# Eighteen weight splits of the Hyena stage move from GpSimd to VectorE

## The chip, the cores and the metric

The kernel runs on one core of a Trainium2 chip. The metric is the time of one execution on the device in microseconds (us). The kernel before takes 3416.87 us, the median of three runs that lie between 3413.32 and 3423.29 us. One execution was taken with the hardware profiler; it took 3412.15 us itself, and its span, from the first to the last recorded instruction, is 3410.4 us.

## The reference

The kernel computes two layers of a diffusion backbone over 1024 latent tokens and 256 context tokens, each of 1024 channels. The first layer runs a bidirectional mLSTM (4 heads) beside a Hyena group of 512 channels; the second is a 2-D neighbourhood attention with 16 heads. Each layer ends in an MLP. What the change touches is the projection `h @ w_in` of the first layer, cut to this:

```python
def project(h, rope):
    q, k, v, o, g, hy = jnp.split(h @ w_in, cuts, axis=-1)
    ...
def combine(hm, o, hy, dtype):
    u, x1, x2 = jnp.split(short_conv(hy, conv_w, conv_b), 3, axis=-1)
    filt = hyena_filters(l_, f_w1, f_b1, f_w2, f_b2, f_w3, f_freq)
    b_out = hyena(u, x1, x2, filt, hy_d)
def hyena(u, x1, x2, filt, dskip):
    z = u
    for o, gate in enumerate((x1, x2)):
        z = gate * (bidir_long_conv(z, filt[:, o, 0], filt[:, o, 1]) + dskip[o] * z)
    return z
```

The long convolution goes through a Fourier transform along the tokens: multiply by the filter's spectrum, transform back, multiply by the gate.

## The kernel before

**Precision by splitting.** A float32 weight tile of 128 x 1024 numbers is written as a sum of a high part `wh`, which is the tile rounded to the TensorE format fp32r, and a low part `wl`, the remainder. Activations are split in the same way. `gemm` (L170) forms each product of three matmuls: L177 and L178 read `wh`, L179 reads `wl`.

**A weight tile's way.** `wload` (L150) asks SyncE's queue (SP) to load 512 KB into `wr` (L155), of which there is one buffer. `split` (L110) then has ScalarE (ACT) cast `wr` into `wh` (L112), and an engine given as `e` subtract `wh` from `wr` into `wl` (L113); with no engine given that is VectorE (DVE). `wh` and `wl` have two buffers each, so a cast waits until TensorE (PE) is done with the tile before last. The next load into `wr` waits until the subtraction has read it. SP's queue is worked in order: what stands behind that load, such as the loads of filter spectra into `Gt` (L618, two buffers) and the stores of staged results (L1050), waits with it.

**The Hyena stage.** It lies between about 205 and 605 us of the span. For each of four groups of 128 channels, three calls of `hy_block` (L578) project u, x1 and x2 with one weight tile each and apply the short convolution: ACT evicts the product (L590, L591), DVE adds the two outer taps (L108). `decimate` (L597) transposes on PE (L605). `hyena_fft` (L609) transforms with small matmuls (L613), and DVE does the butterflies, the multiplication by the spectrum in `Gt` and the butterflies back (L96, L108, tiles `q`, `b`, `s`, `n`). `hyena_gate` (L627) transforms back on PE (L640), and DVE multiplies by the gate out of PSUM (`big<-psf,big`). `gates` (L654) computes the mLSTM gates once, with a weight tile of its own. To give PE more to do, `filler` (L1041) projects some of the mLSTM's q, k, v, o ahead of time: five of its sixteen tiles in this stage, eleven in the mLSTM stage behind it.

**Order.** All instructions are unrolled. A planner sets the order on every engine when the kernel is built, from estimated durations, dependences, buffers and priorities; each engine then runs its own list strictly in that order. The weight loads of `hy_block` have priority "hy" (1000), those of `gates` 60 and those of `filler` 150.

**Who makes `wl` before.** `W_E` (L69) is GpSimd (POOL). It is given to the loads of `hy_block`, `gates`, `filler` and the output projection (L1129, L1161): 12 + 1 + 16 + 8 + 2 = 39 tiles. All other weight tiles, 105 of the same group, are split on DVE. In the Hyena stage POOL has little else to do; the filters that are computed ahead of it also use POOL for some butterflies.

Of the kernel before, what the change touches and what calls it, by code (L numbers as in the profile page):

```python
# [27 lines left out]
def kernel(ctx: ExitStack, tc: tile.TileContext, A, out):  # L28
    nc = tc.nc
    V, S, T, G = nc.vector, nc.scalar, nc.tensor, nc.gpsimd  # L30
# [8 lines left out]
    def mk(pool, shape, tag, bufs, dt=F32):  # L39
        cnt[0] += 1  # L40
        return pool.tile(shape, dt, tag=tag, bufs=bufs, name=f"{tag}_{cnt[0]}")
# [18 lines left out]
    def pr(k):  # L60
        k = HP.get(k, k)
        return ExitStack() if k is None else tc.high_priority(k)
# [3 lines left out]
    PS0, PS1 = dict(g=2, f=2, m=1, t=2, q=1), dict(g=4, f=3, m=1)  # L66
    PS2 = dict(g=3, f=3, m=1, q=1)
    FS, FH, FM = (0, 0, 0), (0, 1, 0, 1, 0, 1, 0, 2), (3, 4, 4)
    W_E = G  # L69

    def psum(**split):

# [16 lines left out]
    def n2(shape=None):  # L89
        return mk(base, shape or [P, 512], "n2", 4)  # L90
# [16 lines left out]
    def stt(o, a, s, b, op0, op1):  # L107
        return V.scalar_tensor_tensor(out=o, in0=a, scalar=s, in1=b, op0=op0, op1=op1)  # L108

    def split(hi, lo, x, e=None):  # L110

        S.copy(hi, x)  # L112
        (e or V).tensor_tensor(out=lo, in0=x, in1=hi.bitcast(F32), op=ALU.subtract)  # L113
# [36 lines left out]
    def wload(at, src, e=None, ks=(0, 8), into=None):  # L150
        with pr(at):
            wp_ = wpool[0]
            raw = mk(wp_, [P, 8, P], "wr", 1)
            r = slice(*ks)
            nc.sync.dma_start(raw[:, r], src)  # L155
            if into is None:
                hi = mk(wp_, [P, 8, P], "wh", 2, F32R)
                lo = mk(wp_, [P, 8, P], "wl", 2, F32R)
            else:
                hi, lo = [mk(into[0], [P, 8 * P], t, into[2], F32R).rearrange("p (k c) -> p k c", c=P) for t in into[1]]  # L160
            split(hi[:, r], lo[:, r], raw[:, r], e)
        for f in msteps[:MS]:
            f()
        del msteps[:MS]
        return hi, lo
# [4 lines left out]
    def gemm(w, h, g, n, M=P, ks=range(8), tag="g"):  # L170

        hi, lo = w
        hh, hl = h
        ps = pt([P, 512], tag)
        ks = list(ks)
        for i, k in enumerate(ks):
            T.matmul(ps[:M, :n], hi[:, k, :M], hh[g][:, k, :n], start=(i == 0), stop=False)  # L177
            T.matmul(ps[:M, :n], hi[:, k, :M], hl[g][:, k, :n], start=False, stop=False)  # L178
            T.matmul(ps[:M, :n], lo[:, k, :M], hh[g][:, k, :n], start=False, stop=(i == len(ks) - 1))  # L179
        return ps  # L180
# [27 lines left out]
    def mod_steps(l, g, pool, bufs, tag):  # L208

        ps = [None]  # L210
        for i in range(16):
            def step(k=i % 8, c0=i // 8 * 256):
                if k == 0 and c0 == 0:
                    ps[0] = pt([P, 512], tag)
                w = mk(pool, [P, 8, P], bufs[0], bufs[1]).rearrange("p (j a) b -> p j (a b)", j=4)
                nc.sync.dma_start(w, A["w_mod"][l, k * P:(k + 1) * P, g * 2048:(g + 1) * 2048].rearrange("p (j c) -> p j c", j=4)[:, :, c0:c0 + 256])
                for j in range(4):
                    T.matmul(ps[0][32 * j:32 * j + 32, c0:c0 + 256], sil[:, k, :], w[:, j], start=(k == 0), stop=(k == 7))
                if k == 7 and c0:
                    mod_end(l, g, ps[0], tag)  # L220
            yield step
# [356 lines left out]
    def hy_block(eb, h, hc, wp):  # L578

        with pr("hb"):  # L580
            w = wload("hy", A["w_in"][eb], W_E)
            hy = mk(wp, [P, BIGN], "big", 5)
            V.memset(hy[:, 0:1], 0.0)
            V.memset(hy[:, 1025:1027], 0.0)
            V.memset(hy[:, 1283:1284], 0.0)
            s = mk(wp, [P, BIGN], "big", 5)
            for g, (t0, n) in enumerate(GR):
                ps = gemm(w, h, g, n)
                o = 1 + t0 if t0 < LAT else 3 + t0
                S.copy(hy[:, o:o + n], ps[:, :n])  # L590
                S.activation(s[:, t0:t0 + n], ps[:, :n], AF.Identity, scale=hc["cw"][:, eb, 1:2], bias=hc["cb"][:, eb:eb + 1])  # L591
            for t0, n, o in ((0, LAT, 0), (LAT, CTX, 1026)):
                for tap in (0, 2):
                    stt(s[:, t0:t0 + n], hy[:, o + tap:o + tap + n], hc["cw"][:, eb, tap:tap + 1], s[:, t0:t0 + n], ALU.mult, ALU.add)
            return s
# [58 lines left out]
    def gates(h, mp, keep):  # L654

        with pr("gt"):
            R = 104

            hi, lo = wload("ga", A["w_in"][12], W_E)
            S.copy(hi[:, :, 32:64], lo[:, :, 0:32].bitcast(F32))  # L660
            sel = mk(mp, [P, 8, P], "q4", 3)[:64, 0, :100]
            nc.scalar.dma_start(sel, A["gsel"])
# [18 lines left out]
            I, F, e, u1, ln, b, ml = [sm[:R, i] for i in range(7)]  # L681
# [30 lines left out]
            eb, emx, me, mp_ = [rows[:, i] for i in range(4)]  # L712
# [34 lines left out]
    def mlstm_consts(pool):  # L747
        rope = mk(pool, [P, 2, LAT], "rope", 1)
        nc.scalar.dma_start(rope, A["rope"])
        mask = mk(pool, [P, 2, P], "mmask", 1)  # L750
        nc.scalar.dma_start(mask, A["mmask"])
        hn = mk(pool, [P, 4], "hn", 1)
        nc.scalar.dma_start(hn, A["hnorm"])
        return rope, mask, hn
# [274 lines left out]
    def split_groups(h, k, src, gr):  # L1029
        for g, (t0, n) in enumerate(gr):  # L1030
            split(h[0][g][:, k], h[1][g][:, k], src[:, t0:t0 + n])
# [6 lines left out]
    h = new_h()  # L1038
    fill = [(hd, j) for hd in range(4) for j in range(4)]

    def filler(n, stage):  # L1041

        with pr("fb"):
            for hd, j in fill[:n]:
                w = wload("fl", A["w_in"][13 + 4 * hd + j], W_E)
                for g, (t0, n_) in enumerate(GR):
                    ps = gemm(w, h, g, n_)
                    st = stage()
                    S.activation(st[:, :n_], ps[:, :n_], AF.Copy, scale=128 ** -0.5 if j == 1 else 1.0)
                    nc.sync.dma_start(early[hd, j, :, t0:t0 + n_], st[:, :n_])  # L1050
            del fill[:n]
# [3 lines left out]
    with tc.tile_pool(name="hp", bufs=1, side="right") as hp:  # L1055
        hc = {}
        stage = lambda: mk(hp, [P, 512], "st", 1)
# [55 lines left out]
    with tc.tile_pool(name="gp", bufs=1, reuse_waits="tile", side="right") as gp:  # L1113
        cst = mlstm_consts(gp)
        with tc.tile_pool(name="ml", bufs=1, reuse_waits="tile") as ml:
            h2 = []
            for g in (1, 2):
                msteps.extend(mod_steps(0, g, ml, ("wm", 2), "n"))

            def load_mixed(k):  # L1120
                with pr("lm"):
                    m_ = mk(ml, [P, BIGN], "big", 13)
                    nc.sync.dma_start(m_[:, :NT], mixd[k])
                    split_groups(h2, k, m_, GR)

            def out1(d):

                with pr("o1"):
                    w = wload("wo1", A["w_out"][d][:, 0:6], W_E, (0, 6))  # L1129
                    for g, (t0, n) in enumerate(GR):  # L1130
                        xp = n2()
                        nc.sync.dma_start(xp[:, :n], A["xT"][:, d, t0:t0 + n])
                        ps = gemm(w, h2, g, n, ks=range(6))
                        stt(xp[:, :n], ps[:, :n], modT[0][:, 16 + d, int(g == 2):int(g == 2) + 1], xp[:, :n], ALU.mult, ALU.add)
                        nc.sync.dma_start(xs[:, d, t0:t0 + n], xp[:, :n])

            mlstm_head(0, gs, ml, cst, lambda k, t: nc.sync.dma_start(mixd[4 + k], t))
            filler(FM[0], n2)
            mlstm_head(1, gs, ml, cst, lambda k, t: nc.sync.dma_start(mixd[4 + k], t))
            filler(FM[1], n2)  # L1140
            last = []
            mlstm_head(2, gs, ml, cst, lambda k, t: nc.sync.dma_start(mixd[4 + k], t))
            filler(99, n2)
            h2.extend(new_h())
            for k in range(6):
                load_mixed(k)
            for d in range(FM[2]):
                out1(d)
            mlstm_head(3, gs, ml, cst, lambda k, t: split_groups(h2, 4 + k, t, GR))
            load_mixed(6)  # L1150
            for d in range(FM[2], 8):
                out1(d)
    gkc.close()
    cst = natten_consts(ctx.enter_context(tc.tile_pool(name="cn", bufs=1, side="right")))
    with tc.tile_pool(name="xg", bufs=1, reuse_waits="tile", side="right") as xp:
# [4 lines left out]
        h = new_h()  # L1160
        w2 = [wload("wo2", A["w_out"][d0:d0 + 4, :, 6:8].rearrange("d p k c -> p d k c"), W_E) for d0 in (0, 4)]  # L1161
        for g, (t0, n) in enumerate(GR):
            for d in range(8):
                hi, lo = [x[:, 2 * (d % 4):2 * (d % 4) + 2] for x in w2[d // 4]]
# [20 lines left out]
    with tc.tile_pool(name="nl", bufs=1, reuse_waits="tile") as nl, \  # L1185
# [29 lines left out]
        for d in range(8):  # L1215
            w = wload("ow1", A["w_o"][d][:, 0:7], E5, (0, 7))
            residual(xg, 1, 0, d, 0, gemm(w, h2, 0, 512, ks=range(7)), 512)
    with tc.tile_pool(name="xg1", bufs=1, reuse_waits="tile", side="right") as xp:
# [3 lines left out]
        hi, lo = wload("ow2", A["w_o"][:, :, 7].rearrange("d p c -> p d c"), E1)  # L1222
# [7 lines left out]
        for d in range(8):  # L1230
            w = wload("ow3", A["w_o"][d], E1)
# [136 lines left out]
```

## Time and profile before

| | before |
|---|---|
| median of three runs | 3416.87 us |
| profiled execution | 3412.15 us |
| its span | 3410.4 us |
| PE busy over the span | 3256.5 us |
| DVE busy over the span | 2056.0 us |
| POOL busy over the span | 355.8 us |
| `wl` made on POOL | 39 instructions, 134.0 us |
| `wl` made on DVE | 105 instructions, 127.5 us |

A row of a group of instructions gives line, engine, operation, output and inputs, shape, count, then busy time, the mean duration of one in ns, and the idle time of the engine just before them with what ended it. A row of the view in order of time gives the start and the duration in us, and in square brackets the idle time of the engine before it with what ended that. "psf", "psg" and "psm" are PSUM tiles. A row of the table of stretches gives, for each engine, busy time and count, then the granted TensorE clock, the share of the DMA engines and GB/s.

### The profile page before, as it was taken

Reading aid. Unit: us, or ns where it says so; the run is one execution under the profiler, and the core shown is the slowest. Engines: PE = TensorE matmul, PEld = TensorE weight load, DVE = VectorE, ACT = ScalarE, POOL = GpSimd, SP = SyncE. Lnnn points to the kernel's source line nnn. Section 1 sums busy time; section 2 is a strip of 40 time slices with the busy share of each in tenths; the row PEclk is TensorE's granted clock in tenths of the full one; section 3 lists DMA queues with packets and bytes.
Section 4 is the critical chain, followed back from the end, with each engine's and each line's share of the span. In section 5 each row is a group of like instructions: output and inputs, shape, how many; then the busy total and the mean of one; then the engine's idle time right before and its main releaser. Section 6 shows DMA issues by size and latency. Waiting matters only on the chain.

```text
span 3410.4 us, 45323 instructions
## 1 busy us (share of the span) xinstructions
PE 3256.5 (95%) x18044; PEld 2652.5 (78%) x18044; DVE 2056.0 (60%) x3655; ACT 1211.5 (36%) x2555; POOL 355.8 (10%) x295
## 2 busy tenths in 40 slices
PE   6889989999989999999999999999999899999999
PEld 4777878777877888788888777777777688888887
DVE  4858979366576445444454776666666755545444
ACT  5742222244343121211111476666665421111111
POOL 0341232101120000000000211111110200000000
PEclk8999999999999999999999999999999999999999
DMA  6432211775632121212111212221224211111111
GB/s 210 151 110 66 72 64 64 256 233 198 204 126 87 61 82 56 93 56 87 56 37 38 78 47 72 69 67 62 70 78 161 68 56 47 47 50 47 47 50 68
DMA packets 140878, 306.12 MB, mean 90 GB/s; under 512 B 12497, under 2 KB 74057, under 8 KB 139258
## 3 DMA queue, kind: packets, MB, share of 16 engines
q1 hardware_dynamic: 131018, 266.60, 23.8%
q0 software_dynamic: 6464, 28.84, 2.8%
q10 hardware_dynamic: 3184, 7.78, 0.7%
q8 instruction: 142, 2.33, 0.3%
q14 instruction: 70, 0.57, 0.1%
HBM read 255.93 MB, written 43.05 MB: 88 GB/s over the span
## 4 chain that ended last, share of the span: by engine, by line
PE 64%; DVE 5%; DMA 4%; ACT 3%; issue 1%; POOL 0%; ACTq 0%; SPq 0%; DVEq 0%; POOLq 0%
PE psg L177 10%; PE psg L178 10%; PE psg L179 10%; PE psf L312 8%; PE psf L313 8%; PE psf L314 8%; DMA wm<-in_w_mod 2%; PE psf L1014 2%; PE psm L999 1%; DVE n L108 1%; PE psf L978 1%; PE psf L979 1%; PE psf L1018 1%; PE psm L1006 1%; DVE h L108 1%
## 5 line engine op out<-in xcount | busy, mean ns | idle before, releaser
L177 PE MATMUL psg<-h,wh 128*128 128x512 f32 (+1 forms) x2728 | 1017.6, 373 | 16.7 <-ACT h L289 8.3
L179 PE MATMUL psg<-h,wl 128*128 128x512 f32 (+1 forms) x2728 | 1009.2, 370 | 10.8 <-POOL wl L113 6.0
L178 PE MATMUL psg<-h,wh 128*128 128x512 f32 (+1 forms) x2728 | 1014.8, 372 | 4.2 <-DVE h L108 3.0
L177 PEld LDWEIGHTS psg<-h,wh 128*128 128x128 f32 x2728 | 518.8, 190 | 111.3 <-issue 16.2
L178 PEld LDWEIGHTS psg<-h,wh 128*128 128x128 f32 x2728 | 519.4, 190 | 100.7 <-issue 14.0
L179 PEld LDWEIGHTS psg<-h,wl 128*128 128x128 f32 x2728 | 518.9, 190 | 101.3 <-issue 10.8
L108 DVE SCALAR_TENSOR_TENSOR x<-psf,modT,x 128x512 f32<-128x512 f32 (+1 forms) x512 | 347.4, 683 | 225.6 <-PE psf L314 225.4
L313 PE MATMUL psf<-al,w2h 128*128 128x512 f32 (+1 forms) x1280 | 473.3, 370 | 0.3 <-DVE al L113 0.3
L314 PE MATMUL psf<-ah,w2l 128*128 128x512 f32 (+1 forms) x1280 | 472.2, 369 | 0.0
L312 PE MATMUL psf<-ah,w2h 128*128 128x512 f32 (+1 forms) x1280 | 470.6, 370 | 0.9 <-ACT ah L112 0.8
L112 ACT CAST w2h<-w2r 128x1024 fp32r<-128x1024 f32 x64 | 67.3, 1052 | 765.8 <-PE psf L313 594.8
L312 PEld LDWEIGHTS psf<-ah,w2h 128*128 128x128 f32 x1280 | 241.7, 189 | 44.5 <-ACT ah L112 3.2
L313 PEld LDWEIGHTS psf<-al,w2h 128*128 128x128 f32 x1280 | 242.0, 189 | 42.1 <-DVE al L113 1.4
L314 PEld LDWEIGHTS psf<-ah,w2l 128*128 128x128 f32 x1280 | 242.0, 189 | 41.3 <-issue 1.2
L112 ACT CAST wh<-wr 128x1024 fp32r<-128x1024 f32 (+2 forms) x144 | 148.6, 1032 | 288.1 <-PE psg L178 225.2
L113 DVE TENSOR_TENSOR wl<-wr,wh 128x1024 fp32r<-128x1024 f32 (+1 forms) x105 | 127.5, 1214 | 151.3 <-ACT wh L112 150.9
L108 DVE SCALAR_TENSOR_TENSOR rr<-psg,rr 128x512 f32<-128x512 f32 x160 | 101.4, 634 | 179.6 <-ACT rr L301 179.6
L113 POOL TENSOR_TENSOR wl<-wr,wh 128x1024 fp32r<-128x1024 f32 (+1 forms) x39 | 134.0, 3436 | 607.2 <-ACT wh L112 554.9
L113 DVE TENSOR_TENSOR w2l<-w2r,w2h 128x1024 fp32r<-128x1024 f32 x64 | 78.3, 1223 | 153.1 <-ACT w2h L112 151.3
L301 ACT ACTIVATE rr<-psg 128x512 f32<-128x512 f32 x160 | 88.1, 551 | 196.6 <-PE psg L179 195.3
L112 ACT CAST ah<-rr 128x512 fp32r<-128x512 f32 x160 | 92.4, 578 | 168.1 <-DVE rr L108 168.1
L113 DVE TENSOR_TENSOR al<-rr,ah 128x512 fp32r<-128x512 f32 x160 | 101.8, 637 | 80.5 <-ACT ah L112 80.3
(295 smaller groups left out, 4329.7 us busy)
## 6 DMA issues: line engine op xcount, KB each, us to landing
wm<-in_w_mod SPq DMA_DIRECT2D x96, 512.0 KB
wr<-in_w SPq DMA_DIRECT2D x64, 512.0 KB
w2r<-in_w SPq DMA_DIRECT2D x64, 512.0 KB
big<-d SPq DMA_DIRECT2D x39, 640.0 KB
TM<-in_rpbT POOLq DMA_DIRECT2D x64, 384.0 KB, 3.4
wr<-in_w_in SPq DMA_DIRECT2D x29, 512.0 KB
wr<-in_w_qkv SPq DMA_DIRECT2D x24, 512.0 KB
d<-b SPq DMA_DIRECT2D x8, 1280.0 KB
```

What stands on the lines that cost most here:

```text
L108: return V.scalar_tensor_tensor(out=o, in0=a, scalar=s, in1=b, op0=op0, op1=op1)
L112: S.copy(hi, x)
L113: (e or V).tensor_tensor(out=lo, in0=x, in1=hi.bitcast(F32), op=ALU.subtract)
L177: T.matmul(ps[:M, :n], hi[:, k, :M], hh[g][:, k, :n], start=(i == 0), stop=False)
L178: T.matmul(ps[:M, :n], hi[:, k, :M], hl[g][:, k, :n], start=False, stop=False)
L179: T.matmul(ps[:M, :n], lo[:, k, :M], hh[g][:, k, :n], start=False, stop=(i == len(ks) - 1))
L301: S.activation(r[:, :n], ps[:, :n], AF.Relu)
L312: T.matmul(ps[:, :n], w2h[:, d], ah[g], start=(i == 0), stop=False)
L313: T.matmul(ps[:, :n], w2h[:, d], al[g], start=False, stop=False)
L314: T.matmul(ps[:, :n], w2l[:, d], ah[g], start=False, stop=(i == 1))
L978: T.matmul(o, Q[hh][:, c0:c0 + P], kx, start=True, stop=False)
L1014: T.matmul(po[64 * hh:64 * hh + 64, rb], Vw[:, rb + j, 64 * hh:64 * hh + 64], pT[hh][0][rb][:, j], start=(j == 0), stop=False)
```

## The change

A second name, `H_E`, is set to `None`, so that `split` falls back to VectorE. The loads of `hy_block` (12 tiles) and `gates` (1 tile) take it in the place of `W_E`. `filler` gets a parameter for the engine: its calls in the Hyena stage give none (5 tiles, VectorE), its calls in the mLSTM stage give `W_E` (11 tiles, GpSimd as before). Eighteen of the 39 subtractions change engine; no operand, size, buffer or priority changes.

```diff
-    W_E = G
+    W_E, H_E = G, None
...
-            w = wload("hy", A["w_in"][eb], W_E)
+            w = wload("hy", A["w_in"][eb], H_E)
...
-            hi, lo = wload("ga", A["w_in"][12], W_E)
+            hi, lo = wload("ga", A["w_in"][12], H_E)
...
-    def filler(n, stage):
+    def filler(n, stage, e=None):
...
-                w = wload("fl", A["w_in"][13 + 4 * hd + j], W_E)
+                w = wload("fl", A["w_in"][13 + 4 * hd + j], e)
...
-            filler(FM[0], n2)
+            filler(FM[0], n2, W_E)
...
-            filler(FM[1], n2)
+            filler(FM[1], n2, W_E)
...
-            filler(99, n2)
+            filler(99, n2, W_E)
```

## The prediction

> **What bounds the kernel now.** I read the page for the whole, then the table of stretches for the stage of the change, then who waits for whom there, and last the order of time on each engine.
>
> ```profile
> span 3410.4 us, 45323 instructions
> PE 3256.5 (95%) x18044; PEld 2652.5 (78%) x18044; DVE 2056.0 (60%) x3655; ACT 1211.5 (36%) x2555; POOL 355.8 (10%) x295
> ```
>
> Over the span PE sets the time and DVE looks free. In the stage it is otherwise:
>
> ```profile
> 285.00:440.00 155.00, 142.69 (x866) 125.56 (x865) 147.09 (x257) 38.58 (x67) 32.06 (x8) 0.99 0.23 75
> 440.00:510.00 70.00, 54.76 (x311) 48.12 (x310) 50.17 (x90) 14.63 (x25) 23.25 (x4) 0.90 0.21 68
> ```
>
> Times are PE, PEld, DVE, ACT, POOL. From 285 to 440 DVE is busy for 147.09 of 155 us and PE loses 12.3; from 440 to 510 PE loses 15.2 of 70. The waits of PE from 205 to 605 us say on whom:
>
> ```profile
> PE psf L640 <- DVE b L96: 18.4, 4, 8.5
> PE psm L605 <- DVE big L108: 10.0, 4, 4.3
> PE psg L179 <- POOL wl L113: 6.0, 2, 5.4
> ```
>
> So in the stage PE stands for DVE's arithmetic, and once for POOL's split. Within 285 to 440 us its single gaps are at most some 2 us:
>
> ```profile
> PE psm L605 <- DVE big L108: 5.7, 3, 2.1
> ```
>
> The splits in question, as a group and singly:
>
> ```profile
> L113 POOL TENSOR_TENSOR wl<-wr,wh x18: 2357/3002/10399, 211.9 to 548.6; 128x1024 fp32r<-128x1024 f32 x18
> ...
> 211.94 2.51 POOL L113 TENSOR_TENSOR wl<-wr,wh 128x1024 fp32r<-128x1024 f32 x1
> ...
> 438.39 8.39 POOL L113 TENSOR_TENSOR wl<-wr,wh 128x1024 fp32r<-128x1024 f32 x1 [20.10 <-ACT wh L112]
> ```
>
> One shape takes 2.36 to 10.40 us. What stretches it is DVE, and it stretches DVE in turn. DVE's groups by shape, 285 to 440 us:
>
> ```profile
> L108 DVE SCALAR_TENSOR_TENSOR big<-big,cw,big 128x1024 f32<-128x1024 f32 x11 | 16.2, 1471 | 0.3 <-ACT big L591 0.3
> L96 DVE TENSOR_TENSOR b<-b,gt 128x1024 f32<-128x1024 f32 x9 | 12.8, 1462 | 0.0
> L96 DVE TENSOR_TENSOR b<-b,q 128x512 f32<-128x512 f32 x16 | 12.2, 819 | 0.0
> L108 DVE SCALAR_TENSOR_TENSOR big<-big,cw,big 128x256 f32<-128x256 f32 x10 | 11.1, 1112 | 0.0
> L96 DVE TENSOR_TENSOR q<-b,gt 128x1024 f32<-128x1024 f32 x8 | 9.4, 1216 | 0.0
> L96 DVE TENSOR_TENSOR n<-q 128x256 f32<-128x256 f32 x16 | 8.1, 546 | 0.0
> L96 DVE TENSOR_TENSOR b<-s 128x256 f32<-128x256 f32 x16 | 6.0, 416 | 0.0
> L96 DVE TENSOR_TENSOR n<-q 128x512 f32<-128x512 f32 x8 | 5.5, 683 | 0.0
> ```
>
> Shapes of one size should cost the same, and some groups are too dear: `b<-b,gt` 1462 against 1216, `n<-q` 546 against 416, `b<-b,q` 819 against 683. A single taps instruction shows the plain cost and the stretched one:
>
> ```profile
> 415.96 2.61 DVE L108 SCALAR_TENSOR_TENSOR big<-big,cw,big 128x256 f32<-128x256 f32 x1
> ...
> 419.16 0.47 DVE L108 SCALAR_TENSOR_TENSOR big<-big,cw,big 128x256 f32<-128x256 f32 x1
> ...
> 485.06 1.28 DVE L108 SCALAR_TENSOR_TENSOR big<-big,cw,big 128x1024 f32<-128x1024 f32 x1 [0.15 <-ACT big L591]
> ```
>
> 0.47 us becomes 2.61 exactly while a split finishes beside it: POOL waits until it gets in between DVE's instructions, then one DVE instruction stands for some 2.1 us. Summed over the groups: 11 x (1471-1280) = 2.1, 9 x (1462-1216) = 2.2, 16 x (819-683) = 2.2, 10 x (1112-470) = 6.4, 16 x (546-416) = 2.1, together 15.0 us of DVE's 147.09: seven stretches.
>
> The slow splits have a second price, on SP's queue:
>
> ```profile
> SPq L155 <- POOL wl L113: 168.3, 17, 36.9
> SPq L1050 <- ACT st L1049: 64.0, 12, 18.5
> SPq L618 <- DVE b L96: 53.3, 17, 13.7
> ```
> ```profile
> 446.81 0.33 SPq L155 DMA_DIRECT2D wr<-in_w_in  x1
> 447.23 1.19 SPq L618 DMA_DIRECT2D gt<-d  x2
> ...
> 498.54 1.18 SPq L618 DMA_DIRECT2D gt<-d  x2
> ```
> ```profile
> 439.77 2.35 DVE L96 TENSOR_TENSOR b<-b,gt 128x1024 f32<-128x1024 f32 x2
> 442.04 2.49 DVE L96 TENSOR_TENSOR b<-b,q 128x512 f32<-128x512 f32 x4
> 451.42 0.69 DVE L96 TENSOR_TENSOR s<-b,gt 128x512 f32<-128x512 f32 x1 [6.88 <-DMA gt<-d]
> ...
> 502.61 0.69 DVE L96 TENSOR_TENSOR s<-b,gt 128x512 f32<-128x512 f32 x1 [6.77 <-DMA gt<-d]
> ```
>
> The split of 438.39 ends at 446.78, 2.3 us after DVE has run dry at 444.53; SP then issues the weight load and, behind it, the spectrum that DVE stands for until 451.42. It is a ring: DVE waits for a load, the load for POOL, POOL for a pause of DVE. It happens again before 502.61. PE pays each time; its longest wait is the first:
>
> ```profile
> 459.55 3.75 PE L640 MATMUL psf<-b,tI 128*128 128x128 f32 x16 [8.47 <-DVE b L96]
> ```
>
> **The change, part by part.** Removed are 18 POOL splits; added are 18 on DVE. What one costs there stands in the rows of the MLP (1060 to 1890 us) and of the attention (1985 to 2640 us), with DVE's wait for the cast in front of it:
>
> ```profile
> L113 DVE TENSOR_TENSOR wl<-wr,wh x30: 1216/1226/1226, 1061.4 to 1858.2; 128x1024 fp32r<-128x1024 f32 x30
> DVE wl L113 <- ACT wh L112: 41.2, 29, 2.5
> ...
> DVE wl L113 <- ACT wh L112: 12.7, 15, 3.1
> ```
>
> 1. *DVE's load, -5.* From 285 to 440 us eight splits (POOL's count there) add 8 x 1.23 = 9.8 us and the 15.0 us of stretching go: 5.2 us less on the engine that PE's 12.3 us wait for. Bounds 0 (PE's other order binds) and -5.2. Outside this stretch DVE has slack, and I count nothing either way.
>
> 2. *The ring, -10.* The slot for the late spectrum comes free with the first `b<-b,gt`, half of 2.35 us after 439.77, at 440.9. Landing takes 451.42-447.23 = 4.2 us, so it could be there at 445.1 and leave 0.6 of DVE's 6.88 us; the same sum holds for the second. That is 12.4 us, if the planner puts the split ahead of these multiplications; if it stands behind `b<-b,q`, SP is as late as now and nothing is gained. The cast had ended when POOL began, at 438.39, so the split is ready then, and weight loads have a high priority; I take -10 of 0 to -12.4.
>
> 3. *The first split, -3.* POOL was held by DVE (and by its own filter butterflies) until 214.45, and PE waited 5.4 us. DVE can follow the cast within one instruction and needs 1.23. Behind it the gates' weights arrive at a time of their own, which takes some back. Bounds 0 and -6.0 (both POOL waits).
>
> 4. *The granted clock, -5.* After each long wait PE runs slowly:
>
> ```profile
> 214.00:220.00 6.00, 5.49 (x14) 4.34 (x15) 2.19 (x8) 0.00 (x0) 0.45 (x1) 0.53 0.96 385
> 460.00:467.00 7.00, 7.00 (x31) 6.22 (x30) 6.24 (x17) 0.58 (x2) 0.00 (x0) 0.61 0.08 32
> 509.00:516.00 7.00, 7.00 (x35) 6.41 (x35) 7.00 (x13) 0.76 (x2) 4.50 (x1) 0.70 0.29 95
> ```
>
> Clock lost: 6 x 0.47 = 2.8, 7 x 0.39 = 2.7, 7 x 0.30 = 2.1, together 7.6 us. It returns where the wait shrinks to a gap like those of 285 to 440, where the clock is 0.99. I take -5 of 0 to -7.6. The Trainium skill ("TensorE: Matmul & The Clock Gate", section "What's actually happening") says the same as a rule: about 3.4 us without work halves the clock until as much busy time has passed. These rows agree; by the rule alone, three returns at half clock for 3.4 us are an estimated 3 x 1.7 = 5.1 us.
>
> 5. *New waits, +5.* DVE takes its list in order. Where the split's turn comes before ACT's cast, DVE stands, and with it what is queued: butterflies that PE's inverse transforms (L640) wait for, and taps for L605. The attention's 29 splits waited 12.7 us, 0.44 each; the MLP's 30 waited 41.2, 1.4 each. For 18 that is 7.9 to 24.7 us. I take 0.44, since there, as here, DVE mixes splits with a long chain of its own, and two thirds of it on the path: +5 of 0 to 24.7. The other side of the same order, a split that DVE reaches late, is covered: PE waited for `wl` twice only, 5.4 of 6.0 us at the first tile, though one split took 10.40 us.
>
> ACT, PE and DMA get no instruction more or less. The fillers of the mLSTM stage and the output projection stay on POOL. Sum: -5-10-3-5+5 = -18 us. The profiled execution's own 3412.15 us (1.75 over its span) becomes 3394; it lies 4.7 under the median, so I forecast 3416.87-18 = **3399 us**.
>
> **Rivals.** A measurement of this kernel tells 0.3%, 10.25 us, from no change: 3406.6 to 3427.1.
>
> *A, the ring stays.* The planner sets splits behind the multiplications, or SP meets another late release. Then terms 2 and most of 4 go: -5-3-2.8+5, about -6: 3411. For it: SP also waited 64 us for staged results and 53 for `Gt` slots, causes this change does not touch.
>
> *B, DVE's queue stands for casts.* ACT's cast itself waits for PE's last use of `wh`:
>
> ```profile
> ACT wh L112 <- PE psg L178: 50.7, 8, 15.7
> ```
>
> At the MLP's 1.4 us, 18 splits cost 24.7 us of a DVE that is the limit, SP is late as now, and only 5.2 come back: +20, 3437. It decides once the waits on the path pass the 23 us of gains, about 1.3 us a split. Against it: casts come when PE ends a block, and taps of that block keep DVE in step with PE (its wait for L591 is 0.3 us).
>
> *C, DVE is simply full.* The Trainium skill ("Perfetto Trace Analysis", section "Identifying the Most-Contended Engine") takes Vector's occupancy as a fair measure of how near that engine is to its limit. As a mechanism here: if the 15.0 us are work and not standing, 147.09 of 155 us leaves no room, and 8 x 1.23 = 9.8 us come on top: 3427. The 0.47 against 2.61 us for one shape speaks against it.
>
> *D, more.* The new plan clears all: -5.2-12.4-6.0-7.6 and no new wait, -31: 3386.
>
> That nothing changes at all is excluded as far as the engine goes, since `e` decides L113 alone.
>
> **Numbers.** Forecast (3390 to 3407) 0.50, A 0.22, B 0.13, C 0.08, D 0.07. Faster: 0.47 + 0.02 of A + 0.07 = 0.56. Slower: 0.12 of B, 0.04 of C, 0.01 from a remade order elsewhere = 0.17. Same: 0.27. The range for 8 in 10 runs from D's neighbourhood, 3383, to C's, 3428; the forecast's own range is 3390 to 3407.
>
> **What would show it.** Right: POOL has no `wl` before some 550 us; the five dear groups fall to 1.22 to 1.28, 0.68, 0.47 and 0.42 us; SP's loads at L155 wait for DVE in the place of POOL; no wait for `gt` over 1 us; PE's longest wait at L640 under 3 us and a clock over 0.95 from 440 to 510; DVE's wait for `wh` near 8 us in the stage. Wrong: that last wait at 20 us or more (B), `gt` still late (A), the groups as dear as before without POOL (C).

## The result, and the profile after

The kernel after takes 3383.02 us, the median of five runs from 3372.65 to 3386.58; the kernel before, beside it, 3417.16 us (3413.32 to 3423.29). The ratio is 0.9891, with a 95% interval of 0.9875 to 0.9907: 34.1 us less. The forecast was 18 us less, 3399. The direction was right; the gain is about twice the forecast's, and the time lies at the lower edge of the range (3383). The same kernel timed again beside other runs took 3380.39 us, 37.8 less than before. Its profiled execution was the quickest of its five, 3372.65 us, so the profiles differ by 39.5 us where the medians differ by 34.1 to 37.8.

The head of the page after:

```profile
span 3370.9 us, 45320 instructions
PE 3239.5 (96%) x18044; PEld 2640.3 (78%) x18044; DVE 2050.1 (61%) x3673; ACT 1211.5 (36%) x2555; POOL 272.2 (8%) x277
```

DVE has 18 instructions more and 6 us less of busy time, although 18 splits are 22 us of work: the others became shorter by 28. Where the time went shows in the table of stretches, cut at the first product of the Hyena stage (L177) and at the mLSTM's first (L831). Before, then after; the first row is the stage, the second the rest of the program:

```profile
208.00:638.00 430.00, 382.87 (x2196) 327.93 (x2197) 320.85 (x575) 100.09 (x178) 97.93 (x32) 0.94 0.28 91
638.00:3410.00 2772.00, 2709.22 (x14758) 2197.53 (x14756) 1592.61 (x2768) 976.06 (x2081) 201.94 (x206) 0.99 0.26 84
```
```profile
207.00:598.00 391.00, 370.18 (x2192) 318.08 (x2193) 313.65 (x594) 100.89 (x178) 14.37 (x14) 0.99 0.31 99
598.00:3370.00 2772.00, 2705.23 (x14762) 2195.51 (x14760) 1593.23 (x2768) 975.82 (x2081) 202.67 (x206) 1.00 0.26 84
```

All of it lies in the stage: 430 us became 391, the rest is 2772 in both. With the same matmuls, PE's idle time fell from 47.1 to 20.8 us (26.3) and its busy time from 382.9 to 370.2 (12.7), at a granted clock of 0.99 in the place of 0.94.

PE's waits after, from 205 to 605 us, answer to the prediction's second fence of waits (18.4, 10.0 and 6.0):

```profile
PE psf L640 <- DVE b L108: 8.1, 3, 4.2
PE psg L179 <- DVE big L585: 5.9, 1, 5.9
PE psf L640 <- DVE b L96: 2.7, 2, 1.7
PE psm L605 <- DVE big L108: 2.5, 2, 2.3
```

The wait for taps (L605) is down from 10.0 to 2.5; the waits at L640 from 18.4 + 1.7 to 10.8, and the longest from 8.5 to 4.2. One more is gone: before, PE stood 5.7 us at the stage's end for other weights (`PE psn L218 <- DMA wm<-in_w_mod: 5.7, 1, 5.7`). In the kernels below this wait follows one thing: it is there, at 5.9 to 6.6 us, in all five in which DVE makes none of the splits of `hy_block` and `filler`, the one without any such split among them (`PE psn L218 <- DMA wm<-in_w_mod: 6.6, 1, 6.6`); and it is gone, or 0.8 us at most, in all seven in which DVE makes them, also where POOL works beside it. So it comes with the splits' standing on DVE's list and not with what POOL does; by which step is not shown. No term of the prediction has it.

DVE's groups by shape after, in the window of the prediction, 285 to 440 us:

```profile
L108 DVE SCALAR_TENSOR_TENSOR big<-big,cw,big 128x1024 f32<-128x1024 f32 x11 | 14.1, 1277 | 0.1
L96 DVE TENSOR_TENSOR b<-b,q 128x512 f32<-128x512 f32 x19 | 11.8, 681 | 0.0
L113 DVE TENSOR_TENSOR wl<-wr,wh 128x1024 fp32r<-128x1024 f32 x8 | 9.7, 1215 | 0.3 <-ACT wh L112 0.3
...
L96 DVE TENSOR_TENSOR b<-b,gt 128x1024 f32<-128x1024 f32 x8 | 9.4, 1215 | 0.0
...
L96 DVE TENSOR_TENSOR n<-q 128x256 f32<-128x256 f32 x16 | 6.0, 415 | 0.0
L108 DVE SCALAR_TENSOR_TENSOR big<-big,cw,big 128x256 f32<-128x256 f32 x10 | 4.7, 474 | 0.0
```

Every dear group is at its plain cost, and the narrow taps fell from 1112 to 474 ns; POOL makes no `wl` before 541.7 us. SP's queue, and the place that answers to the prediction's ring, in order of time (start, duration):

```profile
SPq L155 <- DVE wl L113: 102.0, 13, 13.7
```
```profile
424.43 0.33 SPq L155 DMA_DIRECT2D wr<-in_w_in  x1
430.37 6.40 SPq L618 DMA_DIRECT2D gt<-d  x3
```
```profile
429.13 2.35 DVE L96 TENSOR_TENSOR b<-b,gt 128x1024 f32<-128x1024 f32 x2
431.40 2.49 DVE L96 TENSOR_TENSOR b<-b,q 128x512 f32<-128x512 f32 x4
433.81 0.69 DVE L96 TENSOR_TENSOR s<-b,gt 128x512 f32<-128x512 f32 x1
```

The spectra's loads leave SP at 430.37, 1.24 us after the multiplication that frees their buffer began; before, they left 7.46 us after it (439.77, 447.23). DVE goes on at 433.81 without a wait, and no wait for `gt` is left in the stage.

DVE now waits for ACT's casts, first in the whole stage, then in its first 80 us alone (205 to 285):

```profile
DVE wl L113 <- ACT wh L112: 26.4, 5, 10.8
```
```profile
DVE wl L113 <- ACT wh L112: 24.8, 3, 10.8
```

### The profile page after: what moved, and what is told of

It reads as the page before. It is cut to its first block, busy times and chain, and to the rows that moved or that the text cites. A ratio compares the mean times of both kernels' runs of the same rounds, so it can differ in the third digit from the quotient of the medians.

```text
span 3370.9 us, 45320 instructions
## 1 busy us (share of the span) xinstructions
PE 3239.5 (96%) x18044; PEld 2640.3 (78%) x18044; DVE 2050.1 (61%) x3673; ACT 1211.5 (36%) x2555; POOL 272.2 (8%) x277
## 4 chain that ended last, share of the span: by engine, by line
PE 61%; DMA 3%; DVE 3%; ACT 2%; issue 1%; POOL 0%; ACTq 0%; DVEq 0%; POOLq 0%
PE psg L177 10%; PE psg L178 10%; PE psg L179 9%; PE psf L312 8%; PE psf L313 8%; PE psf L314 8%; DMA wm<-in_w_mod 2%; PE psf L1014 2%; PE psm L999 1%; PE psf L978 1%; PE psf L979 1%; DVE n L108 1%; PE psf L1018 1%; PE psm L1006 1%; PE psm L218 1%
## 5 line engine op out<-in xcount | busy, mean ns | idle before, releaser
L177 PE MATMUL psg<-h,wh 128*128 128x512 f32 (+1 forms) x2728 | 1015.2, 372 | 17.5 <-ACT h L289 8.4
L179 PE MATMUL psg<-h,wl 128*128 128x512 f32 (+1 forms) x2728 | 1005.6, 369 | 11.6 <-DVE big L585 5.9
L177 PEld LDWEIGHTS psg<-h,wh 128*128 128x128 f32 x2728 | 517.0, 190 | 112.0 <-issue 15.9
L179 PEld LDWEIGHTS psg<-h,wl 128*128 128x128 f32 x2728 | 517.1, 190 | 101.4 <-issue 10.8
L178 PEld LDWEIGHTS psg<-h,wh 128*128 128x128 f32 x2728 | 517.4, 190 | 98.0 <-issue 13.6
L112 ACT CAST w2h<-w2r 128x1024 fp32r<-128x1024 f32 x64 | 67.3, 1051 | 766.5 <-PE psf L313 594.4
L113 DVE TENSOR_TENSOR wl<-wr,wh 128x1024 fp32r<-128x1024 f32 (+1 forms) x123 | 149.6, 1216 | 177.5 <-ACT wh L112 177.0
L112 ACT CAST wh<-wr 128x1024 fp32r<-128x1024 f32 (+2 forms) x144 | 148.5, 1031 | 257.3 <-PE psg L178 194.6
L112 ACT CAST ah<-rr 128x512 fp32r<-128x512 f32 x160 | 92.3, 578 | 167.9 <-DVE rr L108 167.9
L108 DVE SCALAR_TENSOR_TENSOR h<-psf,modT,h 128x512 f32<-128x512 f32 x128 | 94.2, 748 | 44.0 <-PE psf L314 44.0
```

## The experiments

Three explanations stood against each other: that POOL's splits cost time at the shared way into memory, by stretching DVE's instructions (theory P of the expectations); that they cost time through SP's queue, by holding the next weight load and what stands behind it (R, the ring); and that neither matters, and the order that the planner made anew is what helped (Q). Beside them stood the size of the price that DVE pays for its own splits. All ratios are against the kernel before on the same chip, whose median there was 3418.0 to 3418.2 us. The diffs are shortened; `ones_wide` stands for a tile of ones spread to the split's shape.

**A floor, and two prices on top of it.** Three kernels go out from the kernel after. In the first, 17 of the 18 splits are left out (the gates keep theirs), and the third matmul reads `wh` in the place of `wl`:

```diff
-            split(hi[:, r], lo[:, r], raw[:, r], e)
+            S.copy(hi[:, r], raw[:, r])
+            x_ = at == "hy" or (at == "fl" and e is None)
+            if not x_: tt(lo[:, r], raw[:, r], hi[:, r].bitcast(F32), ALU.subtract, e)
+            lo = hi if x_ else lo
```

> The changed kernel without the lower parts of 17 weight tiles (12 of hy_block, 5 fillers): they are left out of the computation, the third matmul reads the upper part again, so TensorE does the same work; the gates keep their split on VectorE. Neither GpSimd nor VectorE does anything for them: this is the floor. Theory L (VectorE's busy time in the stage is what counts, whatever fills it): 17 x 1.23 = 21 us less on VectorE, 3363 to 3370. Theory S (a stand-still that the planner did not foresee, on the very instruction that TensorE waits for next, is what costs; planned work of VectorE fits in): 3378 to 3384, the same as the changed kernel within 5 us.

The second gives POOL an instruction of the split's size at its place that does not read `wr`, so that no load into `wr` waits for it; nobody reads its result (the line stands ahead of the last one above):

```diff
+            if x_: tt(lo[:, r], hi[:, r].bitcast(F32), hi[:, r].bitcast(F32), ALU.subtract, G)
```

> As the run without the 17 splits, with one GpSimd instruction of the old shape for each of them, that reads wh twice and writes a tile that nobody reads: the port is shared as before the change, nobody waits for the result, and SyncE's weight load does not wait for it. The lower parts of the 17 tiles are left out of the computation here too. This measures the port alone. S: 20 to 28 us over the run without splits, although VectorE has no splits to do (stretches near 25 us, VectorE busy near 317). L: also 20 to 25 us over it, but from a floor of 3363 to 3370, so 3385 to 3393. Theory R (ring the larger part): under 8 us over it.

The third lets the same instruction read `wr`, so that it holds the next weight load as before's splits did; again nobody reads the result:

```diff
-            if x_: tt(lo[:, r], hi[:, r].bitcast(F32), hi[:, r].bitcast(F32), ALU.subtract, G)
+            if x_: tt(lo[:, r], raw[:, r], hi[:, r].bitcast(F32), ALU.subtract, G)
```

> As the run of the port alone, but the GpSimd instruction reads wr and wh, as the old split did, so the next weight load and what stands behind it on SyncE's queue wait for it; still nobody waits for its result, and the lower parts of the 17 tiles are left out. Against the port alone this measures the ring: by the run with Gt on ScalarE's queue 8 to 12 us more, with VectorE waiting for Gt twice for some 6 us. If the ring needs the order of the kernel before, 0 to 4 us. R: 15 us or more.

They took 3364.93 us (ratio 0.9839, 0.9824 to 0.9853), 3391.09 us (0.9915, 0.9901 to 0.9929) and 3418.42 us (1.0003, 0.9992 to 1.0014). The floor came out where theory L had it (3363 to 3370) and not S. The second lies 26.2 us over it, near what both had. The third lies 27.3 over the second, where 8 to 12 had been expected and 15 or more by R. The stage in the table of stretches, floor, second, third:

```profile
208.00:585.00 377.00, 369.07 (x2197) 317.20 (x2198) 292.67 (x575) 99.64 (x178) 20.80 (x14) 0.99 0.32 104
```
```profile
209.00:611.00 402.00, 375.35 (x2193) 321.49 (x2193) 317.97 (x575) 99.64 (x177) 110.53 (x31) 0.97 0.30 97
```
```profile
208.00:637.00 429.00, 381.60 (x2192) 326.39 (x2193) 319.94 (x576) 99.35 (x178) 100.03 (x31) 0.94 0.28 91
```

From floor to second the stage grows by 25 us, and DVE, with the same 575 instructions, is busy for 25.3 us more. The taps of floor and second, and POOL's instructions in the second (durations: least, median, greatest in ns):

```profile
L108 DVE SCALAR_TENSOR_TENSOR big<-big,cw,big 128x1024 f32<-128x1024 f32 x24 | 30.7, 1278 | 5.4 <-ACT big L591 5.4
L108 DVE SCALAR_TENSOR_TENSOR big<-big,cw,big 128x256 f32<-128x256 f32 x24 | 11.7, 486 | 11.6 <-ACT big L591 11.5
```
```profile
L108 DVE SCALAR_TENSOR_TENSOR big<-big,cw,big 128x1024 f32<-128x1024 f32 x24 | 37.2, 1549 | 5.0 <-ACT big L591 5.0
L108 DVE SCALAR_TENSOR_TENSOR big<-big,cw,big 128x256 f32<-128x256 f32 x24 | 18.8, 783 | 11.0 <-ACT big L591 11.0
```
```profile
L96 POOL TENSOR_TENSOR wl<-wh x17: 1892/2869/18347, 212.6 to 523.7; 128x1024 fp32r<-128x1024 f32 x17
```

The taps alone carry 24 x 0.271 + 24 x 0.297 = 13.6 of the 25.3 us. PE's wait for them appears, where the floor had none:

```profile
PE psm L605 <- DVE big L108: 12.3, 6, 3.3
```

So work that nobody reads, on an engine that has little else to do, costs 26 us: this is the stretching by itself. From second to third the stage grows by another 27 us, DVE's busy time by 2 only. What is new in the third is waiting; PE's, DVE's and SP's:

```profile
PE psf L640 <- DVE b L96: 20.8, 4, 10.0
...
DVE s L96 <- DMA gt<-d: 14.4, 2, 7.9
...
PE psg L670 <- ACT wh L660: 6.1, 1, 6.1
```
```profile
SPq L155 <- POOL wl L96: 175.4, 16, 36.6
```

These are before's waits (18.4 at L640, 13.7 for `gt`, 168.3 in SP's queue) once more, and its time to 0.4 us. That the time fits so closely is in part luck: the 6.1 us at the gates (L670) are not in the kernel before, which has 6.0 at L179 for the splits instead. The unread instruction reads `wr` in the place of one `wh`, and that costs 27 us, because a buffer comes free later. PE's idle time makes 20.7 of them (26.65 to 47.4): 18.2 more at L640, where it waits for the chain behind the late spectra, 6.1 at the gates, 5.9 less at the taps, and small ones; busy time at the lower clock makes the other 6.3.

**What DVE pays for its own splits.** After stands 14 us above the floor in the stage (391 against 377) and 15.5 to 18.1 by the medians. To see what more of them cost, DVE gets a second instruction of the same size behind each of the 18 (times one, in place):

```diff
+            if at in ("hy", "ga") or (at == "fl" and e is None):
+                tt(lo[:, r], lo[:, r].bitcast(F32), ones_wide, ALU.mult, V)
```

> The changed kernel with a second VectorE instruction of the same shape behind each of the 18 splits, which multiplies wl by ones in place and for which TensorE waits: 18 x 1.2 = 22 us more of planned work on VectorE, about what GpSimd's stand-still takes in the run with the added instruction on wl (25 us, 3405.6). L: 15 to 22 us over the changed kernel, 3398 to 3405. S: 0 to 8 us over it, 3383 to 3391, since the planner places it.

3389.86 us (0.9913, 0.9898 to 0.9928), 6.8 to 9.5 over the two medians of after. Its stage, and PE's waits in it:

```profile
207.00:611.00 404.00, 377.57 (x2195) 323.92 (x2196) 334.72 (x612) 100.64 (x178) 15.76 (x14) 0.97 0.30 97
```
```profile
PE psf L640 <- DVE b L96: 9.1, 3, 5.5
...
PE psf L640 <- DVE b L108: 6.3, 3, 4.1
...
PE psm L605 <- DVE big L108: 2.3, 1, 2.3
```

DVE's busy time grew by 21.1 us (313.65 to 334.72) and the stage by 13, but by the medians the kernel is only 6.8 to 9.5 us slower: this set costs a third to two thirds of its length. The first set had raised DVE's time by 21.0 us (292.67 to 313.65) for 14 in the stage, but that is a balance: PE's waits grew by 10.8 us at L640, 5.9 at L179 and 2.5 at L605, and the 6.6 at L218 went. Without that, the first set would cost some 20 us, near its whole length. The 25.3 us of stretching cost all of theirs. So of the two theories in the expectations neither holds alone: L fits the floor, S nearly fits this run. The wait for taps shows a difference between planned work and standing: 2.3 us here, 12.3 with the stretching. The planner knows of an instruction on DVE's list and can set taps ahead of it; that an instruction will stand, it does not know. (The last sentence is argued, not shown, and so is that planned work is cheaper as a rule.)

**The price put back onto the kernel after.** Two kernels keep the split on DVE and let POOL work behind each of the 18. In the first POOL rewrites `wr` and so holds the load, in the second `wl`:

```diff
+            tt(raw[:, r], raw[:, r], hi[:, r].bitcast(F32), ALU.subtract, G)
```

> The changed kernel, with one GpSimd instruction of the old split's shape added behind each of the 18 splits: it subtracts wh from wr in place, into a tile that nobody reads. wl comes from VectorE as in the changed kernel, but GpSimd again shares VectorE's port, and the next weight load again waits for GpSimd. The order of the other engines stays. R and P together: most of the 34 us are lost, 3405 to 3425, with VectorE's stretched instructions back (14 or so of 2.1 us) and Gt late again. R alone: 3400 to 3408. P alone: 3395 to 3410. Q: 3383, since the order stays.

```diff
+            tt(lo[:, r], lo[:, r].bitcast(F32), ones_wide, ALU.mult, G)
```

> As the run with the added instruction on wr, but the added GpSimd instruction multiplies wl by ones in place: it shares the port and TensorE waits for it, while SyncE's weight load does not. So the port's price is back and the ring is not. P: VectorE's 2.1 us stretches return, at 285 to 440 us where it is the limit: 3395 to 3412. R: 3383 to 3390, a few us for the stretches. Q: 3383. The difference to the run on wr is the ring's price with the port's price in both: R says 12 or more, P under 5.

3409.57 us (0.9979, 0.9970 to 0.9988) and 3405.59 us (0.9968, 0.9956 to 0.9980): 22.6 to 29.2 us over after, near the 26.2 of the stretching alone. PE's wait for taps, first and second:

```profile
PE psm L605 <- DVE big L108: 14.9, 7, 2.7
```
```profile
PE psm L605 <- DVE big L108: 11.2, 8, 2.3
```

With DVE's splits kept where they are, most of the gain is lost as soon as POOL works beside them, so a new order alone isn't what helped. Theory Q, which had 3383 for both, falls. But the order has a part in the ring. The first kernel costs only 4 us more than the second, where R had 12 or more: SP stands for POOL there too (179.1 us at L155), yet no wait for `gt` appears. At the place of the ring POOL's instruction lets the load go at 445.90 us, and the spectra behind it leave SP at 450.39, 1.24 us after the multiplication that frees their buffer began, as in the kernel after: the held load held up nothing. So holding the load cost 27 us in the one order and about 4 in the other; it costs much only where something urgent stands behind it and is otherwise ready. That is argued from these two cases.

**How much of the ring is the spectra's.** The loads into `Gt` leave SP's queue for ACT's, once in the kernel before, once in the third kernel of the first group:

```diff
-                nc.sync.dma_start(Gt[:, :, :cn], Gd[o, qd, :, :, c0:c0 + cn])
+                nc.scalar.dma_start(Gt[:, :, :cn], Gd[o, qd, :, :, c0:c0 + cn])
```

> The kernel before, its splits still on GpSimd; only the loads of the filter spectrum (Gt, L618) are issued from ScalarE's queue in the place of SyncE's, so that they no longer stand behind the weight load that waits for the late split. The orders of VectorE and GpSimd stay nearly the same. Theory R (the ring SyncE - GpSimd - VectorE was the largest part): the two waits of VectorE for Gt (13.7 us) and TensorE's 15.2 us behind them go, with most of the half-clock time after them (5.3 us): 12 to 20 us faster than before, 3397 to 3405. Theory P (GpSimd's port, which stretches VectorE's instructions, was the largest part): 0 to 4 us, 3413 to 3417. Theory Q (neither; the planner's remade order gained it): about 3417. Under each, ScalarE's queue may stand for a buffer of Gt and take a few us back.

> As the run with port and ring (3418.4; GpSimd's instruction reads wr and wh, the lower parts of the 17 tiles are left out), but Gt is loaded from ScalarE's queue, so only the weight load itself and the staged stores still stand behind GpSimd. If the two late loads of Gt are the ring: back to within 8 us of the run of the port alone, 3391 to 3399. If the late weight loads count as much (the gates' tile above all, for which TensorE waited 6.1 us): about half way, 3400 to 3409, as in the kernel before with Gt on ScalarE's queue.

3410.01 us (0.9976, 0.9966 to 0.9986), 8.0 less than before; and 3408.95 us (0.9977, 0.9968 to 0.9986), 9.5 less than 3418.42. In both, no wait for `gt` is left and PE's at L640 is down to 4.8 and 2.7 us, yet only 8.0 and 9.5 of the 27 us came back. The 8.0 lie between what R (12 to 20) and P (0 to 4) had expected, the 3408.95 at the slow end of the range (3400 to 3409) that was given for late weight loads that count as much as the spectra. In the first of them the splits tell why: PE's waits, POOL's order of time, and one place of PE's:

```profile
PE psg L179 <- POOL wl L113: 10.9, 4, 5.4
PE psm L605 <- DVE big L108: 7.9, 4, 2.1
```
```profile
438.20 16.91 POOL L113 TENSOR_TENSOR wl<-wr,wh 128x1024 fp32r<-128x1024 f32 x1 [20.01 <-ACT wh L112]
...
482.65 18.91 POOL L113 TENSOR_TENSOR wl<-wr,wh 128x1024 fp32r<-128x1024 f32 x1 [20.20 <-ACT wh L112]
```
```profile
501.61 0.50 PE L179 MATMUL psg<-h,wl 128*128 128x512 f32 x1 [2.72 <-POOL wl L113]
```

Before, the split of 438.39 got through in 8.39 us because DVE ran dry, for want of the spectrum that the split itself held back. With the spectra in time DVE runs on, the same split takes 16.91 us and a later one 18.91, and PE waits for the split. What the pause had cost is partly spent on POOL's longer wait. The second kernel still lies 18 us over the one without the ring (3391.09); there PE stands 7.1 us for evictions (L606) and 4.4 for the gates' weights, and ACT's queue, which now carries the spectra, stands 19.5 us for DVE and 15.8 for PE at L161 before casts. So the ring's 27 us can't be divided by moving the spectra: they carry most of PE's waits in it, and moving them brings other waits. What part the weight loads alone have stays open.

**After once more, and further in its direction.** The kernel after, unchanged:

> The changed kernel once more, beside the runs below, so that they are compared on one chip: 3376 to 3386, 31 to 42 us under the kernel before.

3380.39 us (0.9899, 0.9882 to 0.9915). Then all 39 splits on DVE; that and the filters' butterflies as well; and that and, of every norm, the two blocks of channels that POOL normalizes (it still adds squares):

```diff
-    W_E, H_E = G, None
+    W_E, H_E = None, None
```

> The changed kernel with the remaining 21 splits (11 fillers of the mLSTM stage, 10 tiles of the output projection) on VectorE too. There VectorE is busy 57% of the time and TensorE 96%. P: 8 stretches of 0.3 to 2.1 us go, 0 to 4 us faster than the changed kernel. R: SyncE's queue is less held up, but nothing waited for it long: 0 to 3 us faster. Waits of VectorE for casts: 21 x 0.4 to 1.4 us where it is not the limit, nothing. All: 3378 to 3384.

```diff
-    FE = (G, G, G, G)
+    FE = (None, None, None, None)
```

> All weight splits on VectorE, and the four groups of butterflies of the filters ahead of the stage (FE, eight calls each) on VectorE in the place of GpSimd, which then does not stretch VectorE's chain before the first tile. S and L alike, by what was measured: the all-VectorE kernel was 3372; the first wait of TensorE (5.9 us) shrinks if VectorE's chain ahead of it ends earlier, -2 to -8; VectorE's added work there, 1.7 us for each of 24 to 32 instructions on an engine that is not full, +0 to +6: 3366 to 3376.

```diff
-    ONPOOL = (1, 4)
+    ONPOOL = ()
```

> As the run before this one, and the two channel blocks of every norm that GpSimd normalizes (ONPOOL) go VectorE's way too, while GpSimd still adds squares. At the norms TensorE waits for the first blocks, so shorter latency there counts: GpSimd takes 1.4 us where VectorE takes 0.75, but VectorE does the others in the meantime. -6 to +6 against the run before this one: 3362 to 3380.

3372.16 us (0.9866, 0.9852 to 0.9880), 3372.57 (0.9866, 0.9849 to 0.9883) and 3353.48 (0.9815, 0.9802 to 0.9829). The first and the last gained more than expected (3378 to 3384, 3362 to 3380), the second lies in its range. The remaining 21 splits are worth 8 to 11 us, the butterflies nothing, and the last step 19: the last kernel beats both given ones, before by 64.7 us. Its stage and the rest:

```profile
207.00:598.00 391.00, 375.44 (x2245) 322.61 (x2244) 314.52 (x606) 103.16 (x181) 0.82 (x6) 1.00 0.32 106
598.00:3355.00 2757.00, 2703.75 (x14746) 2196.20 (x14744) 1594.14 (x2818) 963.35 (x2065) 113.60 (x156) 0.99 0.26 84
```

Cut at after's 207 us, the stage is as long as after's and holds 53 matmuls more, though its first product comes only at 213.63 us; the rest is 15 us shorter. Why the rest gains was not taken apart.

## Why the prediction was right and wrong

The floor and the two prices add up: 377 + 25 + 27 = 429, before's 430; 377 + 14 = 391, after's. So the change takes away 25 and 27 us and adds 14, -38 in the stage; the 14 are some 20 for the splits on DVE less some 6 for the wait at L218. The prediction had both causes and the right sign. Its terms for DVE's load, the first split and the new waits make -3 together, where -25 and +20 were measured: -5. Its terms for the ring and the clock make -15, where -27 were measured, and the -6 at L218 it did not have. The step that failed is the ring's size (2); DVE's load came out near its size by luck (1).

1. *DVE's load, forecast -5, measured -25 + 14 = -11, of which some -6 are the wait at L218.* The seven stretches of 285 to 440 us were seen and sized (15.0 us there; the runs' 25.3 over the stage), but the step "Outside this stretch DVE has slack, and I count nothing either way" was wrong on both sides: 25.3 us of stretching go, and 21.0 us of planned work come and cost up to 20. The two errors nearly cancel, which is luck. A stretch costs PE its whole length, here on the taps before L605. Whether planned work may be set off against standing one for one, as the 9.8 were against the 15.0, is not settled: the first set of splits costs near its length, the second a third to two thirds. Of the first set's price 5.9 us lie at one place, the first tile (3, below).

   The Trainium skill ("SBUF — State Buffer", section "Who interferes with whom") states that a VectorE instruction with two SBUF inputs contends with a GpSimd instruction that reads SBUF. The taps and butterflies read two, and the unread POOL instruction stretched them: the trace agrees, with 25.3 us. Another page of the Trainium skill ("Perfetto Trace Analysis", section "Optimizing Scalar/DVE Operations") warns that because of that port, moving work between these two might not help. The runs give it a size: a set of instructions of the splits' size costs 26 us on POOL even without the ring, the splits 15 to 18 on DVE, where the wait at L218 goes with them.

2. *The ring, forecast -10, measured -27, its share of the clock (6.3) among it; with the clock's -5 the forecast was -15.* This is the step that failed. The mechanism that the prediction describes is there: no wait for `gt` is left, and SP's loads wait for DVE. But the term was taken from DVE's wait (12.4 of 13.7 us, rounded down to 10). PE's wait at L640, which the prediction quotes with 18.4 us, is the price on the path, and the ring by itself adds 18.2 there. The rest is other work behind the held load, such as the gates' weights (6.1), and PE's slower clock behind the waits. These 27 us hold for the order without DVE's splits; POOL's hold put back into the kernel after cost some 4. The row of SP's wait, 168.3 us in 17 waits, was used for two of them.

3. *The first split, forecast -3, measured 0.* PE's wait at L179 is 5.9 us; POOL's was 5.4. (Its row names `big L585`, a memset of 0.06 us that stands behind the split on DVE's list.) The cast ends at 207.62 us (`206.58 1.04 ACT L112 CAST wh<-wr 128x1024 fp32r<-128x1024 f32 x1`), and DVE follows at 213.26, after the filters' multiplications and butterflies that stand before it on its list. "DVE can follow the cast within one instruction" forgot that list. With the butterflies on DVE and all splits too, the wait shrinks to 1.1 us, but the stage's first product comes later (213.90 us, against 210.19 with POOL's butterflies and all splits on DVE), and the total is the same.

4. *The granted clock, forecast -5.* PE's busy time fell by 12.7 us for the same matmuls, the clock rose from 0.94 to 0.99. The three places counted held 7.6; the ring alone carried 6.3 and the stretching 6.3 (369.07 to 375.35 between floor and second kernel), and DVE's own splits cost 1.1 of it again (370.18 against 369.07). From 440 to 510 us, where the prediction asked for a clock over 0.95:

```profile
440.00:510.00 70.00, 69.80 (x431) 61.55 (x430) 65.04 (x125) 19.77 (x34) 0.00 (x0) 1.00 0.22 70
```

5. *New waits, forecast +5 from 8 us.* DVE waited 26.4 us for casts, past the 20 that were to speak for rival B; B's price did not come. 24.8 of them lie before 285 us, ahead of the stretch where DVE is the limit, and from there on 1.6 are left. The sign was badly chosen: a wait counts by where it stands. What the splits cost otherwise shows at L640, whose longest wait is 4.2 us where under 3 was asked for.

Rival A (the ring stays) fell with the wait for `gt`, B with the total. C (DVE is simply full) is right on one point, that planned DVE work is not free in this stage, and wrong on the main one: the dear groups fell to their plain cost, so the extra time was standing. D (more) came nearest, at 3386, though by other terms. Its 31 us were the four gains with no price; measured were larger gains and a price of 14.

Open stay what part of the ring the weight loads have, what planned work on DVE costs PE as a rule, by which step the wait at L218 goes, and why the rest of the program gains when POOL normalizes nothing.

## What to carry to other kernels

Work on an idle engine isn't free if it shares a way into memory with an engine on the path: measure it by an unread copy of the instruction, once with the operand whose buffer it holds and once without. The two prices (stretched neighbours, late buffers) can be measured apart; they were of like size here (26 and 27 us), but the second hangs on the order (27 us in one, some 4 in another). Where a queue works in order, price everything behind a held load by the wait of the engine on the path, not by the wait that is seen first. Compare the waits of both kernels in full: a floor can keep a wait that the change takes away, as at L218.

## What the runs showed of the hardware

- A POOL instruction whose median is 2.87 us took up to 18.35 beside a busy DVE (before: up to 10.40 among the 18 splits; with DVE's pauses taken away, 18.91). It did not stand for one DVE instruction but through a row of them, and then held one up for some 2.1 us: beside the split of 438.20 us with 16.91, DVE worked without a pause, and the taps of 452.82 then took 3.37 us in the place of 1.28. The Trainium skill ("SBUF — State Buffer", section "Who interferes with whom") says of a VectorE in its two-port modes that whoever issues first keeps the pair for a whole instruction. That DVE's instructions here run in such a mode no run shows; the 2.1 us are near the 2.36 of a whole split on POOL, and the wait through a row of instructions goes further than that sentence.
- Seventeen such instructions raised DVE's busy time by 25.3 us, some 1.5 each, without one instruction more on DVE.
- A page whose busy shares read DVE 60% before and 61% after hides both: the share counts standing as work (the 25.3 us above).
